# Attention outputs and queries stored in DRAM as high and low parts, and two projections and the attention share of the output projection in 512-column products

## The chip, the cores and the metric

The kernel runs on one core of a Trainium2 chip. The metric is the device time of one execution in microseconds, taken as the median of several executions. PE is the matrix engine, DVE the vector engine, ACT the scalar engine, POOL the general engine, and SP the engine whose queue issues every DMA of this kernel. SP's queue is worked through in order: a DMA that waits for its data or its buffer holds up all that stand behind it.

## The reference, cut to what matters

Two layers over 256 context tokens and 512 latent tokens, width 1024. A layer normalises and modulates the tokens, makes one input projection, feeds its columns to three groups of heads, and joins their outputs in one output projection with a gated residual; an MLP follows. Only the attention group and the output projection meet the change:

```python
aq, ak, av, mq, mk, mv, mo, mi, mf, gq, gk, gv, gg, glr = split_cols(h @ w_in)
q = apply_axial_rope(aq) * HEAD_DIM ** -0.5        # 8 heads of 64; context queries without rope
out_a = window_attention(q, k, av, akc, avc, sink)  # softmax with a sink over window + context
out_m = head_rmsnorm(mlstm both directions) * sigmoid(mo)
out_g = head_rmsnorm(gla both directions) * silu(gg)
x = x + gate * (concatenate([out_a, out_m, out_g]) @ w_out)
```

In the last layer (layer 1) only the latent tokens go on, so attention there has 4 tiles of 128 tokens and not 6.

## The kernel before, in words

Tokens lie along the columns: T = 768, the context in columns 0 to 255 and the latent tokens in 256 to 767. Every matrix product of the projections is made of three products of parts: a float is held as a high part (rounded to the engine's fp32r type) and a low part (what the rounding left), and `mm3` adds high·high, high·low and low·high, so a product over eight k-tiles is 24 matmuls and one over four k-tiles 12. `split(hi, lo, f)` makes the parts: a copy on ACT (line 234) and a subtraction on DVE (line 235).

`H` holds the normalised tokens as such parts, eight k-tiles by 768 columns for each of high and low; `hh` and `hx` are views of it. All input projections read it. When they are done, its k-tiles 0 to 3 are overwritten with the attention outputs and 4 to 7 with those of the other two groups, and the output projection reads it again.

A layer runs so. `proj_T` and `proj_N` load a block of weights, split it, and make products into a ring of two PSUM tiles (`psg`, 512 columns each); the function handed in as `evict` takes a product away. The queries come from `proj_T` as `aq0` and `aq1`, two blocks of 128 rows each, over `halves`: ranges of 256 columns, three in layer 0 and two in layer 1. `ev_q` copies a 256-column piece to `raw`, turns it by the rope (`rope`: three operations on DVE, one on POOL) and stores it to `qdram`. `a_load(pr)` reads a pair of heads back into `qr` and `pair_split` makes of it `qst[0]` (high part of head 0 over its low part) and `qst[1]` (low part of head 1 over its high part): two ACT copies and two DVE subtractions of 64 rows by up to 768 columns. `qst` has two buffers, so one pair is there at a time. For each of 4 pairs and each tile, `a_scores` makes the scores (lines 683 and 690) and the softmax, and `a_values` the outputs; `oa`, 128 rows by 128 tokens, is stored to `adram` (line 742; `NDR` is 4, so the other branch is never taken). Attention takes part in the order with high priority; the projections that follow (mk, mv, mq, gk, gv, gq, and the gates mo and gg) fill PE between its steps.

When attention has ended its memory goes to the two streams `m_stream` and `g_stream` (mLSTM and GLA), again with high priority, one step for each tile; each tile's end is `gated` and `gated_T` (line 869), which writes k-tiles 4 to 7 of `H`. Between their steps PE makes the gates, whose last matmuls (product `gg`, tiles in the order 2, 3, 4, 5, 0, 1) are the last to read the normalised `H`, and then the attention share of the output projection: `at` tiles of 256 columns are loaded from `adram` (line 837) through a ring of four buffers (`st1`, tag "st", also used by the gates' `gate` tiles and by `xc`), split into k-tiles 0 to 3 of `H`, and 8 blocks of 128 rows times each range of `halves` give products of 12 matmuls; each is added to a piece `xc` of the residual, loaded from `xdram` (line 846), changed on DVE (line 850) and stored (line 851). The other share (k-tiles 4 to 7) follows when the streams have ended. The order on each engine is fixed when the kernel is built, by a planner that simulates the engines with costs of its own and lets the higher priority go first; at run time every engine, SP among them, works in that order.

Of the kernel before, what the change touches and what calls it, by code (L numbers as in the profile page):

```python
# [51 lines left out]
NDR = 4  # L52
# [55 lines left out]
def hybrid_backbone(ctx: ExitStack, tc: tile.TileContext, aconst, front, xt, w_ada, w_in, w_out, w_mlp1, w_mlp2, head_bias,  # L108
# [26 lines left out]
    def nx1(shape, name):  # L135
        return stg.tile(shape, F32, tag="nx", name=name, bufs=4)
# [196 lines left out]
    def proj_T(l, name, ranges, evict, na=0):  # L333
# [3 lines left out]
        for m in range(n // P):  # L337
            for t0, t1 in ranges:
# [3 lines left out]
                evict(ps, m, t0, t1)  # L342
# [18 lines left out]
    adram = [dp.tile([4 * P, T], F32, name=f"adram{l}") for l in range(DEPTH)]  # L361
    qdram = [dp.tile([4 * P, T], F32, name=f"qdram{l}") for l in range(DEPTH)]
# [84 lines left out]
    for l in range(DEPTH):  # L447
# [96 lines left out]
        def pair_split(raw, n, dst0, dst1):  # L544

            S.copy(dst0[0:64], raw[0:64])
            V.tensor_tensor(dst0[64:128], raw[0:64], dst0[0:64].bitcast(F32), op=ALU.subtract)
            S.copy(dst1[64:128], raw[64:128])
            V.tensor_tensor(dst1[0:64], raw[64:128], dst1[64:128].bitcast(F32), op=ALU.subtract)

        def ev_k(ps, m, t0, t1):
            n = t1 - t0
            raw = st1([P, 256], "rin")[:, 0:n]
            S.copy(raw, ps)
            if t0 >= NCTX:
                rope(raw, 1.0, t0 - NCTX)
            pair_split(raw, n, kst[0][0][:, t0:t1], kst[1][1][:, t0:t1])
            S.copy(kst[0][1][64:128, t0:t1], raw[0:64])
            V.tensor_tensor(kst[0][1][0:64, t0:t1], raw[0:64], kst[0][0][0:64, t0:t1].bitcast(F32), op=ALU.subtract)
            S.copy(kst[1][0][0:64, t0:t1], raw[64:128])  # L560
            V.tensor_tensor(kst[1][0][64:128, t0:t1], raw[64:128], kst[1][1][64:128, t0:t1].bitcast(F32),
                            op=ALU.subtract)

        def ev_q(base):
            def f(ps, m, t0, t1):
# [6 lines left out]
                dma(qdram[l][(base + m) * P:(base + m + 1) * P, t0:t1], raw)  # L572
# [81 lines left out]
        for b in range(2):  # L654
            proj_T(l, f"aq{b}", halves, ev_q(2 * b), 0)

        with tc.high_priority(HIP):


            def a_load(pr):  # L660
                qr = a2.tile([P, T], F32, tag="qr", name="qr")
                t0 = NCTX if last else 0
                dma(qr[:, t0:T], qdram[l][pr * P:(pr + 1) * P, t0:T])
                qst = [a2.tile([P, T], F32R, tag="qst", name="qst", bufs=NQ) for _ in range(2)]
                pair_split(qr[:, t0:T], T - t0, qst[0][:, t0:T], qst[1][:, t0:T])
# [51 lines left out]
            def a_values(pr, t, pm, a, nl):  # L717
# [23 lines left out]
                if pr < NDR:  # L741
                    dma(adram[l][pr * P:(pr + 1) * P, t * P:(t + 1) * P], oa)
                else:
# [707 lines left out]
```

## Time and profile before

| | us |
|---|---|
| median of 3 runs (lowest, highest) | 1779.75 (1774.22, 1784.72) |
| the profiled execution | 1780.23 |
| its span, first to last instruction | 1778.4 |
| PE busy in the span | 1702.8 |
| DVE busy | 1205.1 |
| ACT busy | 934.9 |

Busy time of PE is no measure of its speed: matmuls overlap, each is listed with its whole length, and the distance from one start to the next is what it costs. The number of instructions in a stretch, beside a stretch in which they follow one another without a gap, tells how much of PE's time was lost. The clock column is the granted clock of PE, 1.00 for 2.4 GHz; a step at the lower level, 1.2 GHz, counts 0.5.

### The profile page before, as it was taken

The numbers are of one execution on the slowest core, as the hardware profiler recorded it, in microseconds if no ns is written. First come the engines' busy times: TensorE is split into PE (matmuls) and PEld (weight loads), VectorE is DVE, ScalarE is ACT, GpSimd is POOL, SyncE is SP. The second block draws the span as 40 slices with busy tenths as digits, with TensorE's granted clock in tenths as the row PEclk, the third lists the DMA queues.
The fourth block names the chain that finished last, engine by engine and source line by source line (L and its number), as shares of the span: only waits on it lengthen the run. The fifth ranks groups of instructions, "written<-read, shape, count | busy, mean of one in ns | idle before, by whom it ended". The sixth has DMA issues, their size and how long they took to land.

```text
span 1778.4 us, 33324 instructions
## 1 busy us (share of the span) xinstructions
PE 1702.8 (96%) x12254; PEld 1541.3 (87%) x12254; DVE 1205.1 (68%) x2603; ACT 934.9 (53%) x2418; POOL 503.2 (28%) x565
## 2 busy tenths in 40 slices
PE   5899999999999999999999988999999989999998
PEld 3799899879878998999999977989888779999997
DVE  5876665587698655655655788666467697667667
ACT  4767777754363432432342467776664444444444
POOL 2210000542043331432342131000342054444441
PEclk8899999989999999999999989999999999999999
DMA  9242324555831422211221313232566713232221
GB/s 371 102 128 65 116 86 130 169 176 181 290 125 48 144 94 95 84 56 64 72 83 42 123 54 99 92 111 83 182 191 210 276 73 107 95 107 95 96 95 60
DMA packets 113362, 216.63 MB, mean 122 GB/s; under 512 B 17544, under 2 KB 65680, under 8 KB 113200
## 3 DMA queue, kind: packets, MB, share of 16 engines
q1 hardware_dynamic: 113200, 214.51, 35.7%
q8 instruction: 97, 1.59, 0.4%
q14 instruction: 65, 0.53, 0.1%
HBM read 189.46 MB, written 25.00 MB: 121 GB/s over the span
## 4 chain that ended last, share of the span: by engine, by line
PE 64%; DVE 8%; ACT 2%; DMA 1%; issue 1%; POOL 1%; SPq 0%; DVEq 0%; POOLq 0%; ACTq 0%
PE psg L263 19%; PE psg L262 19%; PE psg L264 18%; DVE xn L312 2%; DVE wlo L235 1%; PE psg L202 1%; PE psa L202 1%; PE ptr L727 1%; DVE hl L315 1%; PE psc L690 1%; PE pso L731 0%; PE psc L683 0%; PE pso L733 0%; ACT whi L234 0%; PE psm L953 0%
## 5 line engine op out<-in xcount | busy, mean ns | idle before, releaser
L234 ACT CAST whi<-raw 128x512 fp32r<-128x512 f32 (+2 forms) x404 | 265.2, 680 | 345.5 <-PE psg L263 224.2
L235 DVE TENSOR_TENSOR wlo<-raw,whi 128x512 fp32r<-128x512 f32 (+2 forms) x404 | 331.9, 835 | 117.4 <-ACT whi L234 113.5
L263 PE MATMUL psg<-hl,whi 128*128 128x256 f32 (+2 forms) x1216 | 371.6, 306 | 6.6 <-DVE hl L235 3.1
L262 PE MATMUL psg<-hh,whi 128*128 128x256 f32 (+2 forms) x1216 | 369.7, 308 | 6.2 <-ACT hh L234 1.0
L264 PE MATMUL psg<-hh,wlo 128*128 128x256 f32 (+2 forms) x1216 | 367.4, 304 | 1.0 <-DVE wlo L235 1.0
L263 PE MATMUL psg<-ul,whi 128*128 128x512 f32 (+1 forms) x800 | 278.4, 350 | 2.9 <-DVE ul L1287 2.9
L264 PE MATMUL psg<-uh,wlo 128*128 128x512 f32 (+1 forms) x800 | 277.1, 348 | 0.0
L262 PE MATMUL psg<-uh,whi 128*128 128x512 f32 (+1 forms) x800 | 271.8, 351 | 2.6 <-ACT r L1284 1.2
L1155 DVE SCALAR_TENSOR_TENSOR x<-psg,mods,x 128x512 f32<-128x512 f32 (+1 forms) x236 | 146.1, 622 | 153.9 <-PE psg L264 153.6
L263 PEld LDWEIGHTS psg<-hl,whi 128*128 128x128 f32 x1216 | 234.7, 193 | 16.8 <-DVE hl L235 4.7
L262 PEld LDWEIGHTS psg<-hh,whi 128*128 128x128 f32 x1216 | 233.7, 193 | 15.2 <-issue 3.1
L264 PEld LDWEIGHTS psg<-hh,wlo 128*128 128x128 f32 x1216 | 234.3, 193 | 4.5 <-DVE wlo L235 1.4
L262 PE MATMUL psg<-whi,hh 128*128 128x256 f32 (+1 forms) x592 | 172.8, 292 | 5.1 <-DVE vst L235 2.6
L262 PEld LDWEIGHTS psg<-uh,whi 128*128 128x128 f32 x800 | 151.2, 190 | 24.0 <-ACT r L1284 1.7
L264 PE MATMUL psg<-whi,hl 128*128 128x256 f32 (+1 forms) x592 | 170.7, 290 | 0.8 <-POOL hl L320 0.6
L263 PE MATMUL psg<-wlo,hh 128*128 128x256 f32 (+1 forms) x592 | 171.3, 290 | 0.0
L263 PEld LDWEIGHTS psg<-ul,whi 128*128 128x128 f32 x800 | 151.4, 190 | 22.7 <-DVE ul L1287 3.8
L264 PEld LDWEIGHTS psg<-uh,wlo 128*128 128x128 f32 x800 | 151.3, 190 | 19.2
L1286 POOL TENSOR_TENSOR u<-r 128x256 f32<-128x256 f32 (+2 forms) x128 | 120.0, 943 | 81.7 <-ACT r L1284 78.1
L262 PEld LDWEIGHTS psg<-whi,hh 128*128 128x128 f32 x592 | 114.3, 193 | 6.3 <-DVE vst L235 2.7
L264 PEld LDWEIGHTS psg<-whi,hl 128*128 128x128 f32 x592 | 113.7, 193 | 2.2 <-POOL hl L320 1.1
L263 PEld LDWEIGHTS psg<-wlo,hh 128*128 128x128 f32 x592 | 114.1, 193 | 0.5
(326 smaller groups left out, 3386.4 us busy)
## 6 DMA issues: line engine op xcount, KB each, us to landing
raw<-in_w_mlp_dram SPq DMA_DIRECT2D x128, 512.0 KB, 3.2
raw<-in_w_ada_dram SPq DMA_DIRECT2D x96, 512.0 KB, 5.4
raw<-in_w_in_dram SPq DMA_DIRECT2D x40, 512.0 KB, 3.4
raw<-in_w_out_dram SPq DMA_DIRECT2D x16, 512.0 KB, 4.4
gkv<-gndram SPq DMA_DIRECT2D x22, 256.0 KB, 3.2
Mb<-mrow SPq DMA_DIRECT2D x20, 256.0 KB, 3.7
xc<-xdram SPq DMA_DIRECT2D x40, 128.0 KB, 2.1
xdram<-xc SPq DMA_DIRECT2D x40, 128.0 KB, 2.8
```

What stands on the lines that cost most here:

```text
L202: TE.matmul(ps[32 * g:32 * g + 32, :], lhsT=sT[:, k0 + g, :], rhs=raw[:, g, :], start=(k0 == 0), stop=(k0 == 4))
L234: S.copy(hi, f)
L235: V.tensor_tensor(lo, f, hi.bitcast(F32), op=ALU.subtract)
L262: TE.matmul(ps, lhsT=ah(k), rhs=bh(k), start=k == ks[0] and not more, stop=False, **kw)
L263: TE.matmul(ps, lhsT=ah(k), rhs=bl(k), start=False, stop=False, **kw)
L264: TE.matmul(ps, lhsT=al(k), rhs=bh(k), start=False, stop=k == ks[-1], **kw)
L312: V.scalar_tensor_tensor(xn, X[d][:, t0:t1], a, rs, op0=ALU.mult, op1=ALU.mult)
L315: V.scalar_tensor_tensor(lo[:, d, o:o + n], xn, b, hi[:, d, o:o + n].bitcast(F32), op0=ALU.add, op1=ALU.subtract)
L690: TE.matmul(ps, lhsT=q, rhs=kst[kv][b][:, a * P:e * P], start=(b == 0), stop=False, skip_group_check=True)
L727: TE.transpose(pt[:, j, :], pm[w][:, i, j * P:(j + 1) * P], ident)
L1155: V.scalar_tensor_tensor(X[m][:, t0:t1], ps, mods[l][:, kind + m, grp:grp + 1], X[m][:, t0:t1], op0=ALU.mult, op1=ALU.add)
L1286: G.tensor_tensor(u, r, r, op=ALU.mult)
```

## The change

Queries and attention outputs are split into their parts before they are stored, and `adram` and `qdram` hold both parts. `a_load` then consists of four DMAs of 64 rows into `qst`, and the attention outputs are loaded straight into `H`. The queries, gq and the attention share are made in products over `outr` (512 latent columns at once, and 256 context columns in layer 0); eviction goes on in pieces of 256 columns by the new argument `ev`, but for mq, which keeps 512. `ev_k` is written as a loop with the same eight operations in another order.

```diff
-    def proj_T(l, name, ranges, evict, na=0):
+    def proj_T(l, name, ranges, evict, na=0, ev=256):
...
-                evict(ps, m, t0, t1)
+                for a in range(t0, t1, ev):
+                    b = min(a + ev, t1)
+                    evict(ps[:, a - t0:b - t0], m, a, b)
...
-    adram = [dp.tile([4 * P, T], F32, name=f"adram{l}") for l in range(DEPTH)]
-    qdram = [dp.tile([4 * P, T], F32, name=f"qdram{l}") for l in range(DEPTH)]
+    adram = [dp.tile([2, 4 * P, T], F32, name=f"adram{l}") for l in range(DEPTH)]
+    qdram = [dp.tile([2, 4 * P, T], F32, name=f"qdram{l}") for l in range(DEPTH)]
...
+        def parts(raw, n):
+            hl = [nx1([P, 256], nm, F32R)[:, 0:n] for nm in ("hi", "lo")]
+            split(*hl, raw)
+            return hl
...
-                dma(qdram[l][(base + m) * P:(base + m + 1) * P, t0:t1], raw)
+                for i, x in enumerate(parts(raw, t1 - t0)):
+                    dma(qdram[l][i, (base + m) * P:(base + m + 1) * P, t0:t1], x.bitcast(F32))
...
-            proj_T(l, f"aq{b}", halves, ev_q(2 * b), 0)
+            proj_T(l, f"aq{b}", outr, ev_q(2 * b), 0)
...
-                qr = a2.tile([P, T], F32, tag="qr", name="qr")
                 t0 = NCTX if last else 0
-                dma(qr[:, t0:T], qdram[l][pr * P:(pr + 1) * P, t0:T])
                 qst = [a2.tile([P, T], F32R, tag="qst", name="qst", bufs=NQ) for _ in range(2)]
-                pair_split(qr[:, t0:T], T - t0, qst[0][:, t0:T], qst[1][:, t0:T])
+                for h in range(2):
+                    for r in range(2):
+                        o = pr * P + 64 * h
+                        dma(qst[h].bitcast(F32)[64 * r:64 * r + 64, t0:T], qdram[l][h ^ r, o:o + 64, t0:T])
...
-                if pr < NDR:
-                    dma(adram[l][pr * P:(pr + 1) * P, t * P:(t + 1) * P], oa)
...
+                ah, al = [a2.tile([P, P], F32R, tag="oh", name="oh", bufs=4) for _ in range(2)]
+                split(ah, al, oa)
+                for i, x in enumerate((ah, al)):
+                    dma(adram[l][i, pr * P:(pr + 1) * P, t * P:(t + 1) * P], x.bitcast(F32))
...
-        proj_T(l, "gq", halves, ev_gq, 1)
+        proj_T(l, "gq", outr, ev_gq, 1)
...
-        for t0, t1 in halves:
...
+        for t0, t1 in outr:
             for i in range(4):
-                at = st1([P, t1 - t0], "at")
-                dma(at, adram[l][i * P:(i + 1) * P, t0:t1])
-                split(hh[grp][0][:, i, o:o + t1 - t0], hh[grp][1][:, i, o:o + t1 - t0], at)
+                for n in range(2):
+                    dma(H[n].bitcast(F32)[:, i, t0:t1], adram[l][n, i * P:(i + 1) * P, t0:t1])
...
-                for t0, t1 in halves:
+                for t0, t1 in outr:
                     c, grp = m % 2 * P, CTX if t0 < NCTX else LAT
-                    xc = st1([P, t1 - t0], "xc")
-                    dma(xc, xdram[m, :, t0:t1])
                     xh, xl_ = hx(t0, t1)
                     ps = ps_g()[:, :t1 - t0]
                     mm3(ps, lambda k: hi(k, c, c + P), lambda k: lo(k, c, c + P), xh, xl_, range(4))
-                    V.scalar_tensor_tensor(xc, ps, mods[l][:, 16 + m, grp:grp + 1], xc, op0=ALU.mult, op1=ALU.add)
-                    dma(xdram[m, :, t0:t1], xc)
+                    for a in range(t0, t1, 256):
+                        xc = st1([P, 256], "xc")
+                        dma(xc, xdram[m, :, a:a + 256])
+                        V.scalar_tensor_tensor(xc, ps[:, a - t0:a - t0 + 256], mods[l][:, 16 + m, grp:grp + 1], xc,
+                                               op0=ALU.mult, op1=ALU.add)
+                        dma(xdram[m, :, a:a + 256], xc)
```

## Rows read from the trace of the kernel before

**Rows 1.** the profile page, part 1: each engine's busy time and instructions
```profile
PE 1702.8 (96%) x12254; PEld 1541.3 (87%) x12254; DVE 1205.1 (68%) x2603; ACT 934.9 (53%) x2418; POOL 503.2 (28%) x565
```

**Rows 2.** stretches: length, busy us (x instructions) of five engines, clock, DMA, GB/s
```profile
360.00:390.00 30.00, 26.03 (x192) 22.56 (x191) 25.73 (x78) 19.36 (x75) 13.42 (x21) 0.83 0.63 185
390.00:440.00 50.00, 49.60 (x451) 45.52 (x450) 40.38 (x123) 22.77 (x84) 15.91 (x27) 1.00 0.58 178
...
1320.00:1335.00 15.00, 12.80 (x84) 11.16 (x84) 12.47 (x37) 8.72 (x37) 8.11 (x14) 0.77 0.66 202
1335.00:1375.00 40.00, 39.34 (x371) 36.17 (x370) 31.55 (x98) 18.08 (x62) 11.04 (x17) 1.00 0.63 199
```

**Rows 3.** PE timeline, layer 1 MLP: start us, length us, instruction
```profile
1486.99 0.28 PE L262 MATMUL psg<-hh,whi 128*128 128x256 f32 x1
...
1491.31 0.40 PE L262 MATMUL psg<-uh,whi 128*128 128x512 f32 x1
...
1497.91 0.39 PE L264 MATMUL psg<-uh,wlo 128*128 128x512 f32 x1
```

**Rows 4.** PE timeline around the last gg products and the first attention-share products
```profile
344.63 0.28 PE L262 MATMUL psg<-whi,hh 128*128 128x256 f32 x1
...
359.96 0.39 PE L264 MATMUL psg<-whi,hl 128*128 128x256 f32 x1
...
364.95 0.38 PE L262 MATMUL psg<-hh,whi 128*128 128x256 f32 x1 [1.04 <-ACT hh L234]
...
1315.73 0.28 PE L264 MATMUL psg<-whi,hl 128*128 128x256 f32 x1
...
1322.50 0.38 PE L262 MATMUL psg<-hh,whi 128*128 128x256 f32 x1
```

**Rows 5.** SP timeline, layer 0: first and last issues of the at loads
```profile
360.58 0.94 SPq L837 DMA_DIRECT2D at<-adram  x2
...
383.14 1.31 SPq L837 DMA_DIRECT2D at<-adram  x2
```

**Rows 6.** the at tile: ns min/median/max, first and last start us, shapes
```profile
L234 ACT CAST hh<-at x20: 387/404/433, 364.5 to 1333.7; 128x256 fp32r<-128x256 f32 x20
L235 DVE TENSOR_TENSOR hl<-at,hh x20: 410/417/957, 364.9 to 1334.1; 128x256 fp32r<-128x256 f32 x20
```

**Rows 7.** PE and DVE timeline: last gated_T and last xc eviction of each layer
```profile
449.43 0.38 PE L869 MATMUL psl<-ac,g 128*128 128x128 f32 x2
...
457.25 0.48 DVE L850 SCALAR_TENSOR_TENSOR xc<-psg,mods,xc 128x256 f32<-128x256 f32 x1 [1.95 <-DMA xc<-xdram]
...
1377.82 0.38 PE L869 MATMUL psl<-ac,g 128*128 128x128 f32 x2
...
1380.39 0.48 DVE L850 SCALAR_TENSOR_TENSOR xc<-psg,mods,xc 128x256 f32<-128x256 f32 x1 [1.32 <-DMA xc<-xdram]
```

**Rows 8.** the chain that ended last, in order of time: start us, length us
```profile
1096.47 5.12 DMA qr<-qdram
...
1103.00 0.51 PE psc L683 x2
...
1318.59 3.44 DMA at<-adram
```

**Rows 9.** stretch where layer 1 starts attention, columns as in Rows 2
```profile
1100.00:1105.00 5.00, 3.58 (x31) 3.30 (x29) 2.63 (x8) 1.98 (x4) 0.00 (x0) 1.00 0.43 152
```

**Rows 10.** the qr tile: two of its four splits, columns as in Rows 6
```profile
L546 ACT CAST qst<-qr x8: 617/725/842, 106.0 to 1204.1; 64x768 fp32r<-64x768 f32 x4, 64x512 fp32r<-64x512 f32 x4
...
L547 DVE TENSOR_TENSOR qst<-qr,qst x8: 685/818/953, 106.9 to 1205.6; 64x768 fp32r<-64x768 f32 x4, 64x512 fp32r<-64x512 f32 x4
```

**Rows 11.** PE timeline, layer 1: scores before and after a change of pair
```profile
1163.33 0.48 PE L690 MATMUL psc<-kst,qst 128*128 128x256 f32 x2
...
1171.43 0.63 PE L683 MATMUL psc<-kst,qst 128*128 128x256 f32 x4
```

**Rows 12.** the oa tile, columns as in Rows 6
```profile
L739 DVE TENSOR_TENSOR oa<-pso,ob x80: 270/283/285, 129.2 to 1268.8; 64x128 f32<-64x128 f32 x80
```

More of the change, by code (lines that the diff above doesn't have):

```diff
@@ L51 @@
 HIP = 3000
-NDR = 4
 def shape_constants():
@@ L133, in nc1, with nx1 @@
         return stg.tile(shape, dt, tag="nc", name=name, bufs=4)
-    def nx1(shape, name):
-        return stg.tile(shape, F32, tag="nx", name=name, bufs=4)
+    def nx1(shape, name, dt=F32):
+        return stg.tile(shape, dt, tag="nx", name=name, bufs=4)
     def pspool(name):
@@ L556, in ev_k @@
                 rope(raw, 1.0, t0 - NCTX)
[L557 to L562, printed above, removed]
+            for h in range(2):
+                x, own, other = raw[64 * h:64 * h + 64], slice(64 * h, 64 * h + 64), slice(64 - 64 * h, 128 - 64 * h)
+                k0, k1 = kst[h][h], kst[h][1 - h]
+                S.copy(k0[own, t0:t1], x)
+                S.copy(k1[other, t0:t1], x)
+                for k, p in ((k0, other), (k1, own)):
+                    V.tensor_tensor(k[p, t0:t1], x, k0[own, t0:t1].bitcast(F32), op=ALU.subtract)
         def ev_q(base):
@@ L654, in hybrid_backbone @@
         for b in range(2):
-            proj_T(l, f"aq{b}", halves, ev_q(2 * b), 0)
+            proj_T(l, f"aq{b}", outr, ev_q(2 * b), 0)
         with tc.high_priority(HIP):
             def a_load(pr):
-                qr = a2.tile([P, T], F32, tag="qr", name="qr")
                 t0 = NCTX if last else 0
-                dma(qr[:, t0:T], qdram[l][pr * P:(pr + 1) * P, t0:T])
                 qst = [a2.tile([P, T], F32R, tag="qst", name="qst", bufs=NQ) for _ in range(2)]
-                pair_split(qr[:, t0:T], T - t0, qst[0][:, t0:T], qst[1][:, t0:T])
+                for h in range(2):
+                    for r in range(2):
+                        o = pr * P + 64 * h
+                        dma(qst[h].bitcast(F32)[64 * r:64 * r + 64, t0:T], qdram[l][h ^ r, o:o + 64, t0:T])
                 return qst
@@ L740, in a_values @@
                                     op=ALU.add)
-                if pr < NDR:
-                    dma(adram[l][pr * P:(pr + 1) * P, t * P:(t + 1) * P], oa)
-                else:
-                    grp = CTX if t < 2 else LAT
-                    o = t * P - GROUPS[grp][0]
-                    split(hh[grp][0][:, pr, o:o + P], hh[grp][1][:, pr, o:o + P], oa)
+                ah, al = [a2.tile([P, P], F32R, tag="oh", name="oh", bufs=4) for _ in range(2)]
+                split(ah, al, oa)
+                for i, x in enumerate((ah, al)):
+                    dma(adram[l][i, pr * P:(pr + 1) * P, t * P:(t + 1) * P], x.bitcast(F32))
             pend = None
@@ L766, in hybrid_backbone @@
                lambda ps, t: S.copy(mv[:, t, :, 0:64], ps.rearrange("p (h e) -> p h e", h=4)), 1)
[L767 removed]
+        proj_T(l, "mq", outr, lambda ps, m, t0, t1: S.copy(mq[m][:, t0:t1], ps), 1, 512)
         with tc.high_priority(HIP):
```

8 lines of the change are left out of this document (removed).

## The prediction

> **What bounds the kernel now.** I read the page first. PE is listed as busy for 96% of the span [rows 1], but that share adds up overlapping matmuls, so I counted instructions by stretch instead. Where PE runs without a gap it starts about nine instructions per us; the reader should look for stretches with fewer. In the stages that this change touches there are two. From 360 to 390 us (layer 0) 192 instructions stand where the next 50 us hold 451, or 9.0 per us; 30 us at that pace would hold 271, so 79 steps are missing, 8.7 us. From 1320 to 1335 us (layer 1) there are 84 where the following pace of 9.3 per us would give 139: 5.9 us. Together 14.6 us are lost there, with DVE busy for 86% and 83% of the stretch and a clock of 0.83 and 0.77 [rows 2].
>
> The timeline shows what these stretches are. The last gg matmul is at 359.96 and 1315.73, the first one of the attention share at 364.95 and 1322.50, the former held by ACT's split of the first `at` tile [rows 4]. In layer 0 the twelve `at` loads are issued from 360.58 to 383.14, since they go through a ring of four buffers and each waits for the splits before it [rows 5]. So the product is fed at the pace of load, ACT, DVE, buffer free, while the two streams use the same DVE.
>
> Is a gain there kept? That hangs on what ends the stage. The last `gated_T` of the streams is at 449.43 and 1377.82, the last `xc` eviction of the attention share at 457.25 and 1380.39 [rows 7]: the share ends last in both layers, by 7.8 and 2.6 us. What it gains early is kept up to about these sums, and further if the streams too are let go sooner.
>
> **The change, part by part.**
>
> *Products of 512 columns.* Each layer exchanges two 256-column matmuls for one in 4 x 24 = 96 places (queries), 2 x 24 = 48 (gq) and 8 x 12 = 96 (share): 480 in both. From 1486.99 to 1491.31 there are 36 starts of 256 columns, 0.1200 us each; from 1491.31 to 1497.91 29 of 512, 0.2276 us each [rows 3]. A pair saves 0.2400 - 0.2276 = 0.0124 us, in all 6.0 us. The queries and gq stand where PE is dense; the share's pairs (192, 2.4 us) may in part fall where PE waits anyway, so the lower end is 3.6. I take 6. The Trainium skill, "TensorE: Matmul & The Clock Gate", section "Back-to-back issue gap", gives a start-to-start distance of N / 2.4 ns + 2.5 ns: by it a pair saves 2.5 ns, 480 pairs 1.2 us, and my sum would end 4.8 us higher. The trace does not agree at 256 columns (0.1200 against 0.109 us), so I keep the rows.
>
> *Direct loads into `H`.* Gone are 20 `at` tiles with 20 ACT copies of 0.404 and 20 DVE subtractions of 0.417 us [rows 6]: 4.8 and 5.0 us in layer 0, 3.2 and 3.3 in layer 1, out of stretches where DVE is nearly full. Gone too is the ring; the new loads wait for one thing, PE's last read of the rows that they overwrite. In layer 0 the latent columns are free after the fourth of six gg tiles: counted back 48 matmuls from 359.96, near 344.63 [rows 4]. Fifteen us lie between, so these loads can be hidden. In layer 1 all eight wait for 1315.73. The `at` load then took 3.44 us from 1318.59 [rows 8], so the first new one can hardly land before 1319.5 to 1322: the head of that gap stays, its tail (splits up to 1334.1 [rows 6]) goes. The bytes double, 3.1 and 2.1 MB, and SP issues 16 and 8 loads for 12 and 8, at 0.47 us each [rows 5] 1.9 us more of SP; at 200 GB/s, the rate of the stretch [rows 2], the 1.05 MB added in layer 1 take 5 us of DMA, for which the DMA share of 0.66 leaves room in 15 us. Behind a waiting load on SP stand the streams' own loads; that is the third rival. Bounds: nothing, and the whole 14.6 us. I take 5 of 8.7 in layer 0 and 3 of 5.9 in layer 1, about half, since the streams' steps on DVE stay where they are and in layer 1 the first loads are no earlier.
>
> *Eviction of the share.* The same 40 `xc` pieces, two behind each wide product; a product of 12 x 0.228 = 2.7 us covers two evictions of 0.48 us [rows 7]. No cost.
>
> *Queries.* `ev_q` gets a split and a second store per piece, 12 and 8 pieces: 0.40 us ACT and 0.42 us DVE each by the `at` rows [rows 6]. `a_load` loses four operations of 0.62 to 0.95 us [rows 10], so the totals fall a little. At a change of pair the old scores' buffers must be free first; 8.1 us lie between the last scores of one pair and the first of the next [rows 11], enough for four issues of 0.47 us and a landing like that of `qr`, 5.12 us with other loads beside it [rows 8]: no cost, unless that cover falls below 7 us. Only the first pair is exposed. In layer 1 its chain is load at 1096.47, landed at 1101.6, scores at 1103.00 [rows 8]. Taken out are 1.4 us; put in are the split 0.82, one more issue 0.47 and three more for the loads 1.4, and some 1.3 us for 256 KB more at 200 GB/s: 2.6 us later. In layer 0 the two subtractions and two copies taken out weigh 3 us, and it comes out near +1. PE then has other products, but 31 instructions in 5 us [rows 9] show that these don't cover all. I take +2 of this 3.6; the bounds are 0 and +5, the latter if the rope of the second half no longer overlaps a product.
>
> *Attention outputs.* Each of 24 and 16 tiles gets a split of 128 x 128 and a second store. On DVE 128 columns take 0.283 us [rows 12], 256 take 0.417; I take 0.28 there and 0.30 on ACT. That is 14.0 and 9.3 us of the two engines, against the 14.2 and 10.4 us of `pair_split` that go. The split stands behind a finished tile and nobody waits for it until the share, so I count nothing; if it falls into the chain of scores and softmax, it is the third rival. `ev_k`'s order: nothing.
>
> *Sum:* -6 - 8 + 2 = -12 us. The span of 1778.4 becomes 1766.4, the profiled execution of 1780.23 becomes 1768.2. It stands 0.5 us above the median of the runs, so I forecast **1768 us**, own range 1762 to 1771.
>
> **Rivals.**
>
> 1. *The gaps close altogether* (-14.6, start for nothing, -6): 1759.6. For it: the share ends last in both layers, and DVE is relieved exactly there. Against: in layer 1 the share can then end only 2.6 us sooner before the streams are last. 12%.
>
> 2. *The wait is only moved*: PE stands at the share's start for the loads where it stood for the splits, or the streams become the last to end. The gaps give back 2 and the start takes 2; what is left is the 6 of the wider products: 1774. For it: in layer 1 the head of the gap hangs on loads in both kernels, twice the bytes are to come, and the streams lie only 2.6 us below the share. 29%.
>
> 3. *Attention ends later, and with it everything behind it.* The streams begin only when attention has ended. If each tile's split adds its 0.58 us to the chain of ACT and DVE while `pair_split` was in the shadow of those 8.1 us, attention ends 14.0 and 9.3 us later; less the 7.8 and 2.6 us by which the streams may be late [rows 7], 6.2 + 6.7 = 12.9 us are lost, the gap's gain goes under, and with -6 for the width and +3 for the start it is 1790. A load that stands on SP for the last gg tile with the streams' loads behind it has the same effect in layer 0. It turns from harmless to costly once the streams are more than 7.8 and 2.6 us late. Against: the two totals are nearly equal. 15%.
>
> 4. *The width saves nothing*: what a start of 256 columns has above half a start of 512, 0.0062 us, is not saved by joining two. Then the 6 us go and 1774 is left. Against it stand the two runs of starts themselves [rows 3]. 3%. It is the case to which the skill's distance, cited above, comes nearest.
>
> **How the numbers follow.** The forecast has 41%, rival 1 12%, rival 2 29%, rival 3 15%, rival 4 3%. Half a per cent, 8.9 us, is about what a measurement can tell from no change: below 1770.9 is faster, above 1788.6 slower. The forecast and rival 1 are faster (53%), rivals 2 and 4 the same (32%), rival 3 slower (15%). The range reaches down past rival 1 for what DVE's relief may add, and up to part of rival 3: 1757 to 1785.
>
> **What would show each step.** The 512-column steps of the queries should stand at 0.228 us. The layer 0 loads into `H` should be issued before the last gg matmul and the first share product follow it within 2 us; in layer 1 it should still be some 5 us behind. Instructions in the 30 us after the last gg should rise from 192, less one for each pair joined. First scores of layer 1 should come 1 to 3 us later counted from the end of the rope, and attention should last as long as before. The prediction is wrong if the streams start over 8 us later, if the share's products still come in pieces, or if a new gap opens at the change of pairs.

## The result: slower by 2.5%

The changed kernel takes 1822.95 us (median of 4 runs, 1816.76 to 1828.89) against 1778.88 us for the kernel before (4 runs): ratio 1.0252, 95% interval 1.0229 to 1.0275. The prediction said 1768 us, range 1757 to 1785. The profiled span is 1822.4 us against 1778.4, so 44.0 us are to be found.

### The profile after

The page, part 1 (engine, busy us, instructions), which answers to [rows 1]:

```profile
PE 1717.5 (94%) x11774; PEld 1532.5 (84%) x11774; DVE 1194.1 (66%) x2627; ACT 932.4 (51%) x2442; POOL 504.7 (28%) x565
```

PE has 480 matmuls fewer, as counted; DVE and ACT carry a little less, as forecast, and nothing here tells of 44 us. Next, the timeline of PE and DVE: last gg step and first step of the attention share, last `gated_T` and last `xc` eviction, for each layer. It answers to [rows 4, 7].

```profile
354.11 0.28 PE L263 MATMUL psg<-whi,hl 128*128 128x256 f32 x1
354.23 0.39 PE L261 MATMUL psg<-hh,whi 128*128 128x512 f32 x1
...
449.68 0.48 DVE L850 SCALAR_TENSOR_TENSOR xc<-psg,mods,xc 128x256 f32<-128x256 f32 x1
...
482.64 0.44 PE L870 MATMUL psl<-ac,g 128*128 128x128 f32 x2 [1.22 <-DVE hl L234]
...
1317.89 0.28 PE L263 MATMUL psg<-whi,hl 128*128 128x256 f32 x1
...
1320.67 0.50 PE L261 MATMUL psg<-hh,whi 128*128 128x512 f32 x1
...
1368.49 0.88 DVE L850 SCALAR_TENSOR_TENSOR xc<-psg,mods,xc 128x256 f32<-128x256 f32 x2
...
1419.64 0.66 PE L870 MATMUL psl<-ac,g 128*128 128x128 f32 x2 [2.00 <-issue]
```

The gap that the change was to close is closed: the share starts 0.12 us behind the last gg step in layer 0 (before 5.0) and 2.8 us behind it in layer 1 (6.8). The last gg step itself comes earlier, although attention ends later (below): by 5.9 us in layer 0, and in layer 1, counted from that layer's first store of x (999.3 us before, 1025.3 now), by 23.8 us (316.4 and 292.6). But the order of the two ends has turned round. The share ended 7.8 and 2.6 us after the streams; now the streams end 33 and 51 us after the share. SP's timeline of the loads into `H` (first and last issue of each layer; [rows 5] before) shows them in time:

```profile
336.02 0.45 SPq L837 DMA_DIRECT2D hh<-adram  x1
...
358.38 0.32 SPq L837 DMA_DIRECT2D hl<-adram  x1
...
1314.12 0.32 SPq L837 DMA_DIRECT2D hh<-adram  x1
...
1324.24 0.50 SPq L837 DMA_DIRECT2D hl<-adram  x1
```

Now two stages of each layer: from the first scores to the store of the last attention output (the first of its two stores in the changed kernel), and from there to the end of streams and share. Columns as in [rows 2]: length, PE busy (x instructions), four more engines, granted clock. First the changed kernel, with the 30 and 15 us behind the last gg steps and two stretches of layer 1's end, then the kernel before.

```profile
113.50:332.10 218.60, 218.44 (x1740) 199.36 (x1741) 127.25 (x364) 157.28 (x489) 12.88 (x32) 1.00 0.40 124
...
354.10:384.10 30.00, 25.50 (x191) 21.55 (x189) 16.98 (x40) 13.55 (x43) 11.87 (x19) 1.00 0.67 207
...
332.10:482.60 150.50, 131.42 (x1020) 114.08 (x1018) 91.65 (x274) 67.95 (x237) 56.38 (x88) 0.92 0.62 197
1131.10:1310.00 178.90, 178.90 (x1426) 163.56 (x1427) 102.60 (x286) 123.46 (x373) 8.15 (x20) 0.99 0.42 134
1310.00:1419.60 109.60, 92.86 (x706) 78.31 (x704) 66.17 (x199) 49.62 (x168) 43.26 (x68) 0.88 0.62 196
...
1317.90:1332.90 15.00, 15.00 (x134) 11.63 (x133) 8.43 (x26) 7.74 (x28) 8.83 (x14) 1.00 0.94 298
...
1360.00:1370.00 10.00, 8.98 (x76) 6.89 (x76) 7.39 (x21) 5.35 (x15) 3.04 (x4) 1.00 0.81 234
1370.00:1420.00 50.00, 35.91 (x254) 32.62 (x250) 34.15 (x111) 22.48 (x87) 17.21 (x28) 0.74 0.36 113
```

```profile
109.10:314.80 205.70, 205.70 (x1713) 192.29 (x1712) 123.51 (x336) 147.54 (x449) 10.74 (x31) 1.00 0.31 102
314.80:457.70 142.90, 138.19 (x1213) 124.44 (x1212) 101.29 (x291) 79.61 (x266) 57.81 (x89) 0.96 0.62 193
...
1103.00:1269.10 166.10, 165.02 (x1363) 151.12 (x1364) 102.95 (x269) 110.50 (x334) 8.92 (x20) 1.00 0.32 107
1269.10:1380.90 111.80, 107.97 (x967) 96.62 (x967) 74.22 (x216) 65.28 (x205) 46.22 (x70) 0.97 0.65 205
```

Attention lasts 12.9 us longer in layer 0 and 12.8 in layer 1. Its first scores come 4.4 and, in layer 1 counted from its first store of x, 2.1 us later. The stage of the streams changes by +7.6 and -2.2, what follows it by +1.1 and +5.3. These make 44.0 us.

PE's loss stands elsewhere. Attention keeps PE busy with hardly a gap in both kernels (at most 1.1 us of a stage is idle). Taking length less busy times clock as what a stage loses of PE, the streams' stages lost 142.9 - 138.19 x 0.96 = 10.2 and 7.1 us before; now they lose 150.5 - 131.42 x 0.92 = 29.6 and 27.9. That is 40 of the 44 us. In layer 1 nothing but the streams' steps is left for PE after 1370, and for 50 us it is busy for 72% at a mean clock of 0.74. So while attention ran longer PE did not wait; it did projections, and these are missing beside the streams. One step of the projections made by `proj_N` in layer 1's attention, the kernel before and the changed kernel (instructions, then busy us and mean ns):

```profile
L262 PE MATMUL psg<-whi,hh 128*128 128x256 f32 x197 | 57.3, 291 | 0.0
```

```profile
L261 PE MATMUL psg<-whi,hh 128*128 128x256 f32 x241 | 69.7, 289 | 0.0
```

With the other steps of 256 and 512 columns, at 0.12 and 0.2276 us each [rows 3], the projections inside attention take 12.5 us more of PE in layer 1 and 8.9 in layer 0, of the 12.8 and 12.9 us by which attention grew.

Beside the streams PE is idle for 19.1 and 16.7 us (length less busy time; before 4.7 and 3.8). Its longest waits in layer 0's stage are for operands of the streams (PE waits for: us, times, longest); in the kernel before the longest was for the split of an `at` tile, 1.8 us:

```profile
PE psl L1094 <- POOL qd L1086: 4.0, 2, 3.6
PE psl L1094 <- DVE kd L1084: 3.8, 2, 3.6
PE psl L1008 <- ACT qd L1060: 2.5, 1, 2.5
```

In layer 1 the chain that ended last (start, length) runs through transfers too, the share's weights and pieces of the residual among them: 38 us of that stage's chain are DMA, against 7 in the kernel before.

```profile
1327.65 5.18 DMA raw<-in_w_out_dram
...
1345.21 5.24 DMA raw<-in_w_out_dram
...
1354.13 5.98 DMA xdram<-xc
```

Waits of PE in the windows of the two attentions of the changed kernel. There is one in each, and it stands before the very first scores (113.53 and 1131.09 us); at the changes of pair none is listed:

```profile
PE psc L687 <- DMA qst<-qdram: 0.5, 1, 0.5
...
PE psc L687 <- DMA qst<-qdram: 2.7, 1, 2.7
```

### The profile page after: what moved, and what is told of

Same layout as the page of the kernel before. It is cut to its first block, busy times and chain, and to the rows that moved or that the text cites. A ratio compares the mean times of both kernels' runs of the same rounds, so it can differ in the third digit from the quotient of the medians.

```text
span 1822.4 us, 32631 instructions
## 1 busy us (share of the span) xinstructions
PE 1717.5 (94%) x11774; PEld 1532.5 (84%) x11774; DVE 1194.1 (66%) x2627; ACT 932.4 (51%) x2442; POOL 504.7 (28%) x565
## 4 chain that ended last, share of the span: by engine, by line
PE 61%; DVE 7%; DMA 4%; issue 2%; ACT 2%; POOL 1%; SPq 0%; DVEq 0%; POOLq 0%; ACTq 0%
PE psg L261 18%; PE psg L262 18%; PE psg L263 18%; DVE xn L311 1%; PE psa L201 1%; DMA raw<-in_w_out_dram 1%; PE ptr L731 1%; DVE hl L314 1%; DMA xdram<-xc 1%; DMA raw<-in_w_ada_dram 1%; PE psc L694 1%; PE psg L201 1%; DVE wlo L234 1%; PE psm L954 1%; PE psl L1094 1%
## 5 line engine op out<-in xcount | busy, mean ns | idle before, releaser
L234 DVE TENSOR_TENSOR wlo<-raw,whi 128x512 fp32r<-128x512 f32 (+2 forms) x404 | 329.2, 829 | 147.7 <-ACT whi L233 143.9
L261 PE MATMUL psg<-hh,whi 128*128 128x256 f32 (+2 forms) x1056 | 343.2, 330 | 12.0 <-ACT rin L570 3.8
L262 PE MATMUL psg<-hl,whi 128*128 128x256 f32 (+2 forms) x1056 | 343.1, 326 | 3.7 <-DVE hl L314 3.7
L263 PE MATMUL psg<-hh,wlo 128*128 128x256 f32 (+2 forms) x1056 | 342.2, 326 | 1.9 <-DVE wlo L234 1.9
L261 PEld LDWEIGHTS psg<-hh,whi 128*128 128x128 f32 x1056 | 203.3, 194 | 28.1 <-ACT rin L570 4.2
L262 PEld LDWEIGHTS psg<-hl,whi 128*128 128x128 f32 x1056 | 204.5, 194 | 16.7 <-DVE hl L314 4.7
L263 PEld LDWEIGHTS psg<-hh,wlo 128*128 128x128 f32 x1056 | 204.2, 194 | 13.6 <-DVE wlo L234 3.1
L263 PEld LDWEIGHTS psg<-uh,wlo 128*128 128x128 f32 x800 | 151.2, 189 | 19.1
```

Of the source, the lines that this page charges most:

```text
L234: V.tensor_tensor(lo, f, hi.bitcast(F32), op=ALU.subtract)
L261: TE.matmul(ps, lhsT=ah(k), rhs=bh(k), start=k == ks[0] and not more, stop=False, **kw)
L262: TE.matmul(ps, lhsT=ah(k), rhs=bl(k), start=False, stop=False, **kw)
L263: TE.matmul(ps, lhsT=al(k), rhs=bh(k), start=False, stop=k == ks[-1], **kw)
```

## Experiments

The theory after this comparison: the streams' chain (start of scores, attention, streams) has become what the time hangs on; each edit of the change lengthens it, and PE has too little other work beside it. Rivals: one part alone is at fault; the plan of the kernel before is a lucky one; PE's own work has grown.

For every kernel: ratio to the kernel before with its interval, length of attention, issue of the streams' first load (`gkv`) in layer 0, how much later the share ended than the streams, and PE's loss in the streams' two stages worked out as above. Lengths come from one execution each, and ends are read to within 0.5 us. e10, whose order is that of the kernel before, shows how far two executions differ: attention by up to 0.4 us, a stage of the streams by up to 2.8, the stretch between the layers by 3.9. All intervals but those of e10 and e11 lie above 1.

| kernel | median us | ratio | attention | gkv | share end - streams' | lost |
|---|---|---|---|---|---|---|
| before | 1777 to 1780 | | 205.7, 166.1 | 315.2 | +7.8, +2.6 | 17.3 |
| e10 key order alone | 1777.66 | 0.9992 [0.9975, 1.0009] | 205.7, 165.7 | 314.6 | +7.4, +2.7 | 14.7 |
| e11 wide share alone | 1778.14 | 0.9999 [0.9983, 1.0015] | 205.7, 165.7 | 315.2 | -1.2, -2.0 | 19.7 |
| e18 narrow mq, wide share | 1782.95 | 1.0028 [1.0016, 1.0040] | 205.9, 166.0 | 317.5 | -5.1, -4.3 | 25.1 |
| e17 narrow mq | 1784.08 | 1.0034 [1.0021, 1.0046] | 205.8, 165.9 | 316.3 | +12.4, +0.1 | 23.7 |
| e16 wide gq alone | 1785.96 | 1.0040 [1.0024, 1.0056] | 209.1, 176.0 | 320.1 | +12.3, +0.2 | 33.0 |
| e7 all narrow | 1788.61 | 1.0062 [1.0043, 1.0081] | 214.4, 168.6 | 331.6 | -14.3, -2.6 | 23.5 |
| e15 wide queries alone | 1789.93 | 1.0061 [1.0038, 1.0085] | 216.9, 169.6 | 327.5 | -7.8, +0.1 | 29.6 |
| e1 queries' parts alone | 1790.09 | 1.0074 [1.0046, 1.0101] | 212.0, 171.4 | 330.1 | +1.0, +1.3 | 19.3 |
| e2 outputs' parts alone | 1791.07 | 1.0087 [1.0055, 1.0118] | 226.0, 170.0 | 336.4 | -14.7, -2.6 | 26.8 |
| e5 share narrow | 1793.00 | 1.0096 [1.0068, 1.0124] | 217.8, 173.0 | 333.4 | -13.5, -9.4 | 33.1 |
| e12 third buffer | 1793.55 | 1.0077 [1.0041, 1.0114] | 212.7, 169.5 | 329.9 | -3.9, +5.4 | 33.3 |
| e9 half matmuls | 1793.63 | 1.0087 [1.0063, 1.0111] | 218.2, 173.7 | 335.4 | -14.6, -13.3 | 28.2 |
| e4 outputs raw | 1796.55 | 1.0110 [1.0082, 1.0138] | 216.3, 167.7 | 332.6 | -14.1, -5.2 | 33.0 |
| e3 widths alone | 1806.27 | 1.0156 [1.0129, 1.0182] | 220.0, 175.5 | 327.9 | -10.2, -10.1 | 43.8 |
| e8 split on POOL | 1806.83 | 1.0174 [1.0152, 1.0196] | 218.7, 171.7 | 334.1 | -31.7, -27.4 | 39.4 |
| e6 queries narrow | 1814.11 | 1.0208 [1.0186, 1.0231] | 214.4, 178.6 | 331.5 | -31.3, -29.2 | 46.1 |
| after | 1822.95 | 1.0252 [1.0229, 1.0275] | 218.5, 178.9 | 334.5 | -33.0, -51.2 | 57.5 |
| e13 after, share twice | 1829.56 | 1.0287 [1.0254, 1.0321] | 218.3, 172.0 | 336.5 | +1.2, -2.5 | 8.1 |
| e14 before, share twice | 1836.11 | 1.0310 [1.0283, 1.0337] | 205.7, 166.1 | 314.1 | +35.6, +30.7 | 10.9 |

### One part alone

**e1, queries' parts**, in the kernel before:

```diff
+                for i, x in enumerate(parts(raw, t1 - t0)):
+                    dma(qdram[l][i, ...], x.bitcast(F32))
...
+                        dma(qst[h].bitcast(F32)[64 * r:64 * r + 64, t0:T], qdram[l][h ^ r, o:o + 64, t0:T])
```

> The kernel before with only the queries kept as high and low parts (split before the store, four loads a pair straight into the operand); attention outputs raw, all products as before. The changed kernel's attention ended 17.2 us (layer 0) and 17.0 us (layer 1) later than before, 4.3 us of it at its start. Theory Q (the queries' path makes attention late: the loads into the operand can't begin until the last scores of the pair before have read it): attention 10 us or more longer in each layer and the time 1795 to 1815 us. Theory O (the split of each output tile, 0.3 us on ScalarE and 0.3 us on VectorE for 24 and 16 tiles, with two stores, sits on the chain): first scores up to 4 us later, the length of attention within 3 us of before, time 1779 to 1786 us. Theory W (512-column filler products stand in front of the scores on TensorE): length as before, time within 5 us of before.

**e2, outputs' parts**, in the kernel before; the raw queries come in two halves to make room:

```diff
+                split(ah, al, oa)
+                    dma(adram[l][i, ...], x.bitcast(F32))
...
+                    dma(H[n].bitcast(F32)[:, i, t0:t1], adram[l][n, i * P:(i + 1) * P, t0:t1])
...
+                for a in (t0, t0 + n):
+                    dma(qr, qdram[l][pr * P:(pr + 1) * P, a:a + n])
+                    pair_split(qr, n, qst[0][:, a:a + n], qst[1][:, a:a + n])
```

> The kernel before with only the attention outputs kept as high and low parts (split of each tile, two stores, loads straight into H), the share still in 256-column products; for room on the chip the raw queries are loaded and split in two halves of a pair. Theory O: attention 10 to 14 us longer in each layer, the streams end last and the time is 1795 to 1815 us. Theory Q: attention within 3 us of before, the share starts at once behind the gate products, and the time is 1765 to 1780 us. Theory W: as Q.

**e3, widths** (queries, gq, share), in the kernel before:

```diff
-            proj_T(l, f"aq{b}", halves, ev_q(2 * b), 0)
+            proj_T(l, f"aq{b}", outr, ev_q(2 * b), 0)
-        proj_T(l, "gq", halves, ev_gq, 1)
+        proj_T(l, "gq", outr, ev_gq, 1)
-                for t0, t1 in halves:
+                for t0, t1 in outr:
```

> The kernel before with only the widths changed: queries, GLA queries and the attention share in 512-column products, evicted in pieces of 256. Theory W: a filler product holds TensorE 0.23 us instead of 0.12 us at a time and the psum of a group is released later, so that attention is 10 us or more longer in each layer and the time 1790 to 1810 us. Theories Q and O: attention within 3 us of before in length, the start of scores up to 3 us later since the eviction of the first 512 columns waits for the whole product, and the time 1770 to 1782 us (up to 6 us of shorter products).

**e4, outputs raw again**, in the changed kernel:

```diff
-                split(ah, al, oa)
-                for i, x in enumerate((ah, al)):
-                    dma(adram[l][i, ...], x.bitcast(F32))
+                dma(adram[l][pr * P:(pr + 1) * P, t * P:(t + 1) * P], oa)
```

> The changed kernel with the attention outputs raw again (one store a tile, loads into a staging tile and a split ahead of the share, as before); queries in parts and the widths as in the changed kernel. Theory O: attention's length back within 3 us of before, the time 1778 to 1790 us. Theory Q: attention as in the changed kernel (12.9 us longer), the time 1815 to 1830 us. Theory W: as Q. If each part has its share, the length lies between and the time is 1795 to 1810 us.

None of the theories that named one part held. Each part alone is slower, by 0.7, 0.9 and 1.6%, and each makes attention longer; without the outputs' part 19 of the 44 us are still there. For what fills attention, one group of the costliest in layer 0's attention, kernel before and e2 (instructions, then busy us and mean ns):

```profile
L262 PE MATMUL psg<-whi,hh 128*128 128x256 f32 x235 | 67.9, 289 | 0.0
```

```profile
L262 PE MATMUL psg<-whi,hh 128*128 128x256 f32 x280 | 80.7, 289 | 0.0
```

The three steps of the product grow from 235, 235 and 234 to 280, 279 and 279: 134 matmuls at 0.12 us [rows 3], 16 of the 20.3 us by which attention grew. Which of them run inside attention is the planner's choice, and each of these kernels has another order; no run added the work of a part and kept the order. e2 also loads and splits the queries in halves, so its numbers aren't the outputs' alone.

### Which width

**e5**: the changed kernel with the share over `halves`. **e6**: with only aq over `halves`. **e7**: with all three over `halves`.

```diff
-                for t0, t1 in outr:
+                for t0, t1 in halves:
```

> The changed kernel with the attention share in 256-column products again; the direct loads, the queries in parts and the queries' 512-column products stay. The widths alone cost 28 us, and in layer 0 the streams took 145 us with them against 127 to 134 us without. Theory W-share (between the streams' steps PE holds each of them up behind products twice as long, and the share is spent in half as many pieces): attention as in the changed kernel (218.6 and 178.9 us), the streams of layer 0 back at some 134 us from 148.1, the time 1800 to 1810 us. Theory W-queries (the wide query products lengthen attention): as the changed kernel, 1818 to 1830 us.

> The changed kernel with only the queries' products (aq0, aq1) at 256 columns again. Theory W-queries: attention 7 us or more shorter in each layer than in the changed kernel (218.6 and 178.9 us), the time 1800 to 1812 us. Theory W-share: attention within 3 us, the streams of layer 0 still 145 us or more, the time 1815 to 1830 us.

> The changed kernel with all three products (queries, GLA queries, share) at 256 columns, so the queries and the outputs in parts together. If the parts add up as they did alone (13 us for the outputs, 12 us for the queries): 1800 to 1806 us. If the costs of the two are one and the same wait, counted twice when each is alone: 1788 to 1795 us. If the widths are harmless beside them: 1818 us or more.

The share's width costs 30 us in the changed kernel, the queries' 9; e6 fits neither theory well. Narrow, queries and outputs in parts cost 11.6 us together, no more than either alone, so the parts' costs can't be added.

**e9**: the changed kernel with wide groups, but each matmul issued as two.

```diff
+                            for a in range(0, t1 - t0, 256):
+                                TE.matmul(ps[:, a:a + 256], lhsT=u(k, c, c + P), rhs=v(k)[:, a:a + 256], ...
```

> The changed kernel with the attention share still in groups of 512 columns in one psum tile, evicted in two pieces behind the group, but each 512-column matmul issued as two of 256. With the share wholly in 256-column groups the time was 1793.0 us, 29.5 us less. Theory grain (the cost of the wide share is the time that a streams' step waits for the matmul in front of it, 0.228 us and not 0.120 us): 1790 to 1800 us, layer 0's streams 134 us. Theory group (the cost lies in the two evictions together, with two loads and two stores of xc behind each product, and in the psum tile held twice as long): 1815 to 1830 us, the streams 145 us or more.

Its two stages of the streams:

```profile
332.90:467.00 134.10, 125.62 (x1115) 114.01 (x1114) 90.93 (x274) 67.92 (x237) 54.74 (x88) 0.96 0.70 220
...
1286.10:1387.00 100.90, 89.77 (x829) 80.29 (x829) 68.16 (x199) 51.60 (x173) 43.75 (x69) 0.96 0.71 224
```

The grain (the length of one matmul) decides. Group, psum tile, loads and evictions are the changed kernel's, PE's order in layer 0 up to the end of attention is the same, as in e5 and e13, attention there is as long (218.2) and the streams start within 1 us; but from there to the end it is 134.1 us and not 150.5, and 29.3 us are back in all. From there on the plan was made anew, so what the longer matmul costs at run time and what it does to the order aren't told apart.

**e11, e15, e16**: in the kernel before, the share alone, the queries alone, gq alone at 512 columns (the lines of e3).

> The kernel before with only the attention share in 512-column products. Its share begins after attention has ended in each layer. Theory share: start and length of attention as before in layer 0 (109.1 and 205.7 us), the streams 8 us or more longer in layer 0, the time 1790 to 1805 us. If the streams' late start is needed for the loss (with the streams first, the share ends last and hides them): streams up to 8 us longer but the time within 6 us of before, 1774 to 1784 us.

> The kernel before with only the queries' products (aq0, aq1) at 512 columns. All widths together cost 28 us, the share's alone nothing, so what is left lies with the queries, with the GLA queries, or in several together. Theory queries (attention gets longer since the queries of the later pairs come in larger pieces among its steps): attention 10 us or more longer than 205.7 and 166.1 us, the streams 10 us later, the time 1790 to 1806 us. Theory together (any one of the widths is covered by the 8.3 and 2.6 us by which the share ends after the streams): 1775 to 1782 us.

> The kernel before with only the GLA queries' products (gq) at 512 columns. gq stands among the attention steps as filling. Theory queries: attention within 2 us of before, the time 1775 to 1781 us. Theory filling (512-column products among the steps of attention hold each step up for up to 0.11 us more, and gq alone suffices): attention 5 us or more longer, 1785 us or more.

The wide share alone neither costs nor gains (0.9999): it ends 6.8 us sooner, its streams take 136.4 us against 134.2, and they are last by 1.2 and 2.0 us. The queries and gq cost 10 and 6 us alone, with attention 11.2 and 3.5, 3.4 and 9.9 us longer. All three together cost 28. So in layer 0 the same wide share lengthens the streams by 2 us where they start at 315 and by 14 to 16 us where they start at 333 to 335 (against e5 and e9).

### A lucky plan?

**e10**: the kernel before with only the new order of `ev_k`'s eight operations. **e17**: with mq at 256 columns. **e18**: e17 and the wide share.

```diff
-        proj_T(l, "mq", outr, lambda ps, m, t0, t1: S.copy(mq[m][:, t0:t1], ps), 1)
+        proj_T(l, "mq", halves, lambda ps, m, t0, t1: S.copy(mq[m][:, t0:t1], ps), 1)
```

> The kernel before with the reordered key eviction alone: the same eight operations on ScalarE and VectorE, so no work is added or taken away; but the order that the planner writes down for the later stages comes out different. In every kernel so far, whichever part was in it, the streams of layer 0 started at 328 to 336 us, where the kernel before starts them at 315. Theory plan (the kernel before is a lucky order, and any edit ahead of attention loses it): attention of layer 0 212 us or more against 205.7, the streams' start 325 us or later, the time 1785 to 1795 us. Theory parts (each part has its own cost): 1774 to 1781 us and the streams' start within 3 us of before.

> The kernel before with the mLSTM queries (mq), the one projection that it makes in 512-column products while attention goes on, in products of 256. The GLA queries made 512 wide alone lengthened attention by 3.4 and 9.9 us and cost 6.3 us. Theory filling (a wide product among the attention steps makes attention longer): attention 2 us or more shorter than 205.7 and 166.1 us, the streams earlier by as much; since the share then ends last by more than 8.3 us, little of it can be kept: 1768 to 1778 us. Rival (it is not the width but that the plan around attention changes, which costs here as it did there): attention 3 us or more longer, the time 1782 to 1792 us.

> The kernel before with mq in 256-column and the share in 512-column products: the two widths that theory filling prefers, the share being wide where the streams leave it room. Alone, the wide share ended 6.8 us sooner in layer 0 and gained nothing, the streams being last then. Theory filling: attention as in the run with mq alone, the share's gain kept as the streams start earlier, 1764 to 1776 us, the fastest of all. Rival as there: 1782 us or more.

e10's first attention:

```profile
108.40:314.10 205.70, 205.70 (x1712) 192.26 (x1711) 123.55 (x336) 147.55 (x450) 10.67 (x30) 1.00 0.32 102
```

e10 made no new plan: PE's 12254 matmuls have the same tiles in the same order as in the kernel before, and so have the instructions of DVE, ACT and POOL. So it shows that this edit is free and doesn't test the luck theory. e17 tests it in part. PE's order is another in both attentions, its work hardly more (96 pairs at 0.0124 us, 1.2 us), attention is as long as before, and the time is 0.3% longer. So another order can cost some 6 us; that it alone makes attention 13 us longer no run shows or excludes, and no variation is clearly faster than the kernel before. My idea falls that any 512-column product among attention's steps lengthens it: with mq narrow attention stayed as it was. e18 was to be the fastest of all and was not.

### Two remedies that did not reach far

**e8**: in the changed kernel the split of the outputs on POOL. **e12**: e1 with a third `qst` buffer.

```diff
-                split(ah, al, oa)
+                G.tensor_copy(ah, oa)
+                G.tensor_tensor(al, oa, ah.bitcast(F32), op=ALU.subtract)
...
-NQ = 2
+NQ = 3
```

> The changed kernel with the two operations of each output tile's split moved from ScalarE and VectorE to GpSimd, which was busy for only 13 of the 219 us of attention in layer 0. Theory O-engine (the split takes ScalarE and VectorE from the softmax's chain, 0.58 us a tile): attention 8 us or more shorter in each layer, the time 1800 to 1812 us. Theory O-store (it is the second store of each tile and the wait of the queue of stores that cost, not the engines): attention within 3 us of the changed kernel's, the time 1815 to 1830 us.

> The kernel before with the queries in parts (1790.1 us, attention 212.0 and 171.4 us long) and a third buffer for the loaded queries, so that half of a pair's loads can be issued before the pair ahead of it is done. Theory Q-wait (the loads that stand behind the last scores of a pair make attention longer): attention 3 to 6 us shorter in each layer, the time 1780 to 1785 us. Theory plan: attention within 2 us of that without the buffer or changed without regard to the pairs' ends, the time 1786 to 1795 us.

POOL gives 16 us back; attention is 7.2 us shorter in layer 1 but the same in layer 0, so only half of the theory's sign is there. The third buffer gains nothing, which agrees with the waits above: the loads at the change of pairs are not what makes attention longer.

### Is TensorE short of work?

**e13, e14**: every product of the share made twice, in the changed kernel and in the kernel before.

```diff
-                    mm3(ps, ...)
+                    for _ in range(2):
+                        mm3(ps, ...)
```

> The changed kernel with every product of the attention share made twice into the same psum tile (the second replaces the first), with the same loads and evictions. By the rows that is 8 x 12 x (0.2276 + 0.1200) = 33.4 us of TensorE in layer 0 and 8 x 12 x 0.2276 = 21.8 us in layer 1, 55 us in all. In the two stages from the last store of an attention output to the end of streams and share, the changed kernel loses 54 us of TensorE at full clock (idle, or at the lower clock); the kernel before loses 16. Theory streams (the streams end last and TensorE has too little else to do): the added work fits in, the time stays within 15 us of the changed kernel's, 1810 to 1838 us. Rival (TensorE's work is the bound, and wide products cost more than they seem): 1865 to 1880 us.

> The kernel before with every product of its share made twice: 8 x 12 x 5 x 0.1200 = 58 us of TensorE. It loses only 16 us in these stages, so theory streams expects 35 to 58 us more than before, 1812 to 1837 us; the rival that TensorE always has room beside the streams: under 1800 us.

The two stages of the streams in e13:

```profile
334.10:485.80 151.70, 148.77 (x1186) 130.83 (x1185) 95.64 (x271) 68.99 (x237) 56.14 (x88) 1.00 0.60 185
...
1305.70:1421.50 115.80, 111.76 (x834) 91.89 (x833) 69.86 (x199) 52.39 (x173) 44.20 (x69) 0.99 0.62 195
```

Some 55 us more of PE's work cost the changed kernel 6.6 us (1829.56 - 1822.95); some 58 us cost the kernel before 56.4 (1836.11 - 1779.71), with attention's order unchanged. In the one PE had time to spare, in the other its work was the bound. The test isn't quite clean: in e13 layer 1 has another order, with attention 6.9 us shorter and the streams' stage 6.2 longer than in the changed kernel; but by the stages too, 1.2 and 6.2 us longer, most of the 55 us fitted in.

## Why the prediction was wrong

Rival 3 came true in its mechanism: attention ended later, the streams became last. I had given it 15% and 1790 us. Two steps failed, and the loss needs both.

**The first step that failed** is "The split stands behind a finished tile and nobody waits for it until the share, so I count nothing", with "attention should last as long as before". The sizes were right: the tile `oh` (ns min/median/max; answers to [rows 12])

```profile
L233 ACT CAST oh<-oa x40: 282/300/332, 139.2 to 1309.7; 128x128 fp32r<-128x128 f32 x40
L234 DVE TENSOR_TENSOR oh<-oa,oh x40: 273/281/697, 140.4 to 1310.2; 128x128 fp32r<-128x128 f32 x40
```

shows 0.300 and 0.281 us against 0.30 and 0.28. But I asked who waits at run time. The order was fixed beforehand; in it attention's steps stand farther apart, with more projections between them, and PE works through them without a wait. No idle time marks the loss where it arises. e2 shows the step in the kernel before (attention 20.3 and 3.9 us longer, 13 us lost, the halved loads of the queries included), e4 takes it out of the changed kernel (attention 2.2 and 11.2 us shorter, 26 us back); e1, e15 and e16 show its counterparts for the queries and the widths. It doesn't carry the 44 us alone: in e5 and e9 layer 0's streams start as late, and with a narrow grain of the share they lose 16 and 15 us.

**The second: the width**, -6 us by 480 pairs at 0.0124, wrong in sign. A 512-column start is still 0.23 us in the changed kernel, so a pair saves what I said; the step wrongly took PE's work to be what sets the end. The widths alone cost 28 us (e3), in the changed kernel the share's grain 29 (e9), beside streams that start in time nothing (e11).

**The direct loads**, -8: the gap closed further than forecast (0.12 us against "within 2" in layer 0, 2.8 against "some 5" in layer 1), in the 30 us behind the last gg step the clock rose from 0.83 to 1.00 and DVE's busy time fell from 25.7 to 17.0 us. There PE's busy time taken at full clock rose from 21.6 to 25.5 us, in the 15 us of layer 1 from 9.9 to 15.0: 9.0 us, against the 8 forecast, so the size was right. The share ended 7.6 us sooner in layer 0. None of it was kept, since "the share ends last in both layers" no longer held.

**The queries' start**, +2: measured +4.4 and +2.1. Layer 1's 2.6 was nearly right, layer 0's 1 was short. The chain of layer 1's first scores (start, length), which answers to [rows 8]:

```profile
1120.41 5.06 DMA qdram<-hi
...
1128.10 2.86 DMA qst<-qdram
...
1131.09 0.48 PE psc L687 x2
```

"No cost" at the change of pairs was right as a wait: PE's waits for queries, 0.5 and 2.7 us, stand before the first pair and belong to this term, and e12 agrees. The eviction of the share held PE for 1.1 us in layer 0, as good as the forecast nothing.

**Rival 3's price.** It made the streams 14.0 and 9.3 us late. Their first loads came 19.3 us late in layer 0 (334.5 against 315.2) and 12.7 in layer 1 (285.6 against 272.9, from its first store of x). Less the 7.8 and 2.6 us of cover, that is 11.5 + 10.1 = 21.6 us. It also took their length as given; they grew from 134.2 to 148.1 and from 105.6 to 108.8 us, 17.1 more, and 6.4 us follow behind the stage. With these the rival's sum is 45 and the measured one 44.0, the rest being where an end is read.

**Open.** How a small addition makes the planner set attention's steps farther apart, above all why gq, which attention doesn't read, added 9.9 us in layer 1. Why a wide share lengthens late streams by 14 to 16 us and early ones by 2: shown is that the grain decides, not how much of it is a step waiting behind a matmul, how much another order, how much the lower clock, and how much the share's own loads and stores on SP's queue, which stand in layer 1's chain; e9 keeps these and gets 29 us back, but in another order. The streams being last is not the whole of it in the small edits: in e1, e16 and e17 the share still ends last or beside them, and yet 12, 6 and 7 us are lost. In e1 the scores begin late, by 5.8 us in layer 0 and, counted from the end of layer 0's streams and share, 6.2 in layer 1. In e16 and e17 layer 1's share has lost its lead: in every kernel where it ends at least 1 us behind the streams (before, e1, e10, e12, e14) 397 to 398 us follow, in all others, e16 and e17 among them, 401 to 405. So a lost lead goes with some 3 to 8 us more behind the stage; what they consist of is open. And no version faster than the kernel before was found.

## What to carry to other kernels

Where a high-priority chain is filled up with other work by a planner, the chain's ends can decide, and time added to it shows up not as a wait but as filling used up too early: compare when each chain starts and ends, and how much filling is left beside the last one. Before counting a saving on the filling, see by how much it ends after the chain; here the cover was 7.8 and 2.6 us. To learn which of two is the bound, double the filling: it cost 6.6 us in the one kernel and 56.4 in the other.

## What the runs showed of the hardware

PE's granted clock fell when only the streams' steps were left in layer 1 of the changed kernel: 1.00 in the 10 us before 1370, a mean of 0.74 in the 50 us after (a mean between 0.5 and 1.00 mixes the two levels, 1.2 and 2.4 GHz). The same sixteen matmuls of the streams took 1.16 us with filling in front (clock 1.00 from 430 to 440 us) and 1.91 us at the end of layer 0 (clock 0.65 from 470.6 to 473.6), in the chain of the changed kernel:

```profile
435.01 1.16 PE psl L1094 x16
...
471.01 1.91 PE psl L1094 x16
```

So PE's idle time came with a second cost, longer steps of the streams themselves. In e13, with the gap filled by work that serves nothing, the clock of these stages was 1.00 and 0.99, and the streams of layer 0 took no longer (147.7 us against 148.1).
